# One re-searched instruction order for a 3x3 convolution with 2x2 max-pooling: head casts and evacuations on other engines, four stores cut into halves

## The chip, the core and the metric

The kernel runs on one core of one Trainium2 chip. The metric is device time in microseconds (us), as the median of several executions. The core has a matrix engine (TensorE, PE in the profile, with its weight loads as PEld), VectorE (DVE), ScalarE (ACT), GpSimd (POOL) and SyncE (SP). Each engine takes its instructions from its own queue. [...]

## The reference

```python
batch, c_in, h, w, c_out, k = 16, 64, 64, 64, 128, 3
x_pad = np.pad(x, ((0, 0), (0, 0), (1, 1), (1, 1)))
for b, co, ci, kh, kw:                      # five nested loops
    conv[b, co] += weight[co, ci, kh, kw] * x_pad[b, ci, kh:kh+h, kw:kw+w]
output[b, c, i, j] = max of the 2x2 block of conv[b, c] at rows 2i, 2i+1 and columns 2j, 2j+1
```

Input and output are fp32: 16 images of 64 channels with 64x64 pixels in, 16 images of 128 channels with 32x32 pixels out.

## The kernel before

**Tiling.** Two images lie side by side on the 128 partitions (2 x 64 channels). The work is cut into 32 steps, numbered 0 to 31; a step is a quarter of one such pair, that is 16 input rows or 8 row pairs. Within a step, `h` is 0 or 1, one of the two images; a product of `h` uses 64 rows of the PE array, so products of both images run beside each other in the two halves of the array. Each product is three matmuls (the three column taps) with a moving operand of 64x512 or 64x504 elements into one PSUM tile `acc` of 128x512 fp32. There are eight such tiles ("banks"), all of PSUM, handed out by a queue `free`.

**Even and odd rows.** Of a row pair the kernel needs the larger of the two convolution rows only. So a bank `ta` gets what one row has for itself, a bank `tb` what the other has, the larger of both is taken first, and what both have in common is added after that. A step is of one of two types (`TYPES`):

- K (10 steps): the input is cast to bf16 (`kx`); products `PA1`, `PA2` fill `ta`, `PB1`, `PB2` fill `tb`, `PR` adds the common part from a row sum `KS`.
- W (22 steps): row differences `E` and `D` and a row sum `WS` are made of the fp32 input `wx`. `P2` fills `ta`, `SE` copies it to `tb`, `P0` adds to `ta`, `P3` to `tb`, `P1` adds the common part.

**The steps of the order**, as the texts below name them (`MX.31.1` is `MX` of step 31, image 1):

| step | line | engine | work |
|---|---|---|---|
| `EV` | 439, 441 | ACT | copies bank `ta` to `ev` in SBUF and frees it |
| `SE` | 451 | ACT | copies `ta` to `tb` |
| `MX` | 467 | DVE | `tb` = max(`tb`, `ev`) |
| `OD` | 471 | ACT | copies the odd columns of `tb` to `od` |
| `CM` | 477 | DVE | `o` = max(even columns of `tb`, `od`), frees `tb` |
| `ST` | 485, 487 | SP (`ST.31.0`: ACT) | store of `o` |
| `WS` | 339, 352, 360 | DVE | row sum: with the odd rows copied to PSUM by `XC` on ACT (`ODD_ROWS_IN_PSUM`), as a reduction (`SUM_BY_REDUCTION`), or from two SBUF operands |
| `E`, `D` | 372, 381 | POOL; `E` of `DIFF_ON_VECTOR` on DVE | row differences |
| `KS` | 320 | DVE | row sum of a K step |
| `L`, `LB`, `LK` | 112, 101 | SP; `LK` POOL | loads; `LB` and `LK.0.0` wait for an earlier DVE step |

**The head.** The nine taps of the weights (`wraw`) are cast and combined into seven blocks (D2, G0, D0, G2, GM, G1, GP). `g0`, `g1`, `g2`, `D2`, `D0`, `GS`, `GM`, `GP` compute them, `u..` on POOL copies one 64-column slot, `T..` transposes a block on PE into a bank (line 170), `V..` evacuates the bank into `wt` as bf16 (lines 182 to 188). Step 0 is loaded as fp32 in two parts (`kfirst`) and cast row parity by row parity (`XOa`, `XOb`, `XEa`, `XEb`, line 492); its products `F.k.part` are half products of both images. `X1` and `X2` cast the second quarter (`ksecond`). Step 1, the first W step, is computed in halves too: `Ea`, `Eb`, `Da`, `Db`, `G.k.part`, `SEa`, `SEb`. Which engine does a head step is set by `TURNED_BY_SCALAR`, `CAST_BY_SCALAR`, `TAPS_BY_VECTOR` and `SUMS_BY_GPSIMD`. Eight dummy matmuls (line 595) keep PE busy until the weights have come.

**The order.** The kernel does not let the framework schedule. A string `ORDER` names every step in program order; each engine executes its own steps in that order, and waits by semaphores for what they depend on. Products are queued in two lanes, one for each image, and are emitted in pairs as soon as both lanes hold one. Before, the string ends with

```
... OD.29.1 CM.29.0 OD.31.0 CM.29.1 OD.31.1 ST.29 CM.31.0 ST.31.0 CM.31.1 ST.31.1
```

Of the kernel before, what the change touches and what calls it, by code (L numbers as in the profile page):

```python
# [11 lines left out]
def kernel(  # L12
# [467 lines left out]
    def store(s, h=None):  # L480
        p, q = place[s]
        dst = out[2 * p : 2 * p + 2, :, q * R : (q + 1) * R, :].rearrange("b c h w -> c b (h w)")
        src = ot[s].rearrange("p b h w -> p b (h w)")
        if h is None:
            nc.sync.dma_start(out=dst, in_=src)
        else:
            (nc.scalar, nc.sync)[h].dma_start(out=dst[:, h : h + 1], in_=src[:, h : h + 1])
# [46 lines left out]
    for m in PRODUCTS:  # L534
        steps[m] = lambda s, h, m=m: product(m, s, h)

    ORDER = """
# [5 lines left out]
        SE.3.0 P1.1.0 MX.1.1 MX.2.1 PR.2.0 P0.3.1 EV.3.1 P3.3.1 OD.1.0 P1.1.1 L.16 L.17 P0.3.0 MX.3.1 P3.3.0
        OD.2.0 EV.3.0 ST.0 CM.2.0 PR.2.1 OD.1.1 E.4 CM.1.0 MX.3.0 P1.3.1 PA1.5.1 PA1.5.0 L.15 PB1.5.0 PA2.5.1
        OD.2.1 E.11 P1.3.0 PB2.5.0 XC.6 PA2.5.0 L.12 CM.1.1 OD.3.1 XC.4 CM.2.1 CM.3.1 P2.4.0 PA1.7.0 P2.4.1
        OD.3.0 WS.6 EV.5.1 PB1.5.1 E.6 CM.3.0 WS.4 PA2.7.0 SE.4.1 EV.5.0 PB2.5.1 KS.5 KS.7 SE.4.0 WS.9 P0.4.1
        MX.5.1 P0.4.0 PA1.7.1 ST.3 P3.4.1 LK.1.0 EV.4.1 MX.5.0 EV.7.0 P3.4.0 PA2.7.1 MX.4.1 XC.8 EV.4.0 PR.5.1
        PR.5.0 EV.7.1 P2.6.0 PB1.7.0 OD.5.1 E.8 MX.4.0 OD.5.0 P1.4.1 CM.5.1 P1.4.0 PB1.7.1 CM.5.0 OD.4.1 PB2.7.1
        D.6 P2.6.1 PB2.7.0 SE.6.0 D.9 P2.8.1 OD.4.0 CM.4.1 WS.8 P0.6.0 SE.6.1 P3.6.0 MX.7.1 MX.7.0 PR.7.0 P2.8.0
        PR.7.1 D.8 EV.6.0 CM.4.0 OD.7.1 MX.6.0 SE.8.1 P0.6.1 CM.7.1 P3.6.1 P1.6.0 E.9 EV.6.1 LK.1.1 P0.8.1 L.20  # L550
        P3.8.1 MX.6.1 P1.6.1 D.11 P2.9.0 OD.7.0 SE.8.0 P2.9.1 CM.7.0 EV.8.1 ST.5 P0.8.0 OD.6.0 SE.9.0 P3.8.0
        MX.8.1 OD.6.1 CM.6.0 P1.8.1 P0.9.0 CM.6.1 L.22 EV.8.0 SE.9.1 P2.11.0 KS.13 MX.8.0 P3.9.0 E.12 P1.8.0
        PA1.13.1 OD.8.1 PA2.13.1 L.19 EV.9.0 SE.11.0 CM.8.1 EV.13.1 L.24 D.12 P0.9.1 OD.8.0 P3.9.1 P2.12.1
        P0.11.0 P3.11.0 WS.11 PA1.10.1 PA2.10.1 MX.9.0 P1.9.0 EV.9.1 PA1.13.0 EV.11.0 ST.4 CM.8.0 XC.14 ST.2
        MX.9.1 OD.9.0 SE.12.1 MX.11.0 P1.9.1 P2.11.1 WS.14 PA2.13.0 P1.11.0 EV.10.1 P0.12.1 EV.13.0 PA1.10.0
        E.14 OD.9.1 CM.9.0 P2.14.0 OD.11.0 SE.11.1 WS.12 CM.9.1 EV.12.1 P3.12.1 P0.11.1 D.14 PB1.10.1 CM.11.0
        E.15 P3.11.1 PA2.10.0 E.19 SE.14.0 EV.11.1 P2.12.0 KS.10 MX.12.1 E.17 PB2.10.1 L.23 P1.12.1 P0.14.0
        SE.12.0 MX.11.1 P1.11.1 P3.14.0 EV.14.0 XC.22 MX.14.0 EV.10.0 P0.12.0 WS.22 P2.14.1 MX.10.1 ST.1 P3.12.0
        E.20 EV.12.0 P1.14.0 OD.14.0 MX.12.0 PB1.13.1 OD.12.1 OD.11.1 PB1.10.0 CM.14.0 PB2.10.0 ST.6 P1.12.0
        CM.12.1 PB2.13.1 E.16 CM.11.1 PR.10.1 SE.14.1 P0.14.1 PA1.21.0 MX.13.1 ST.11 XC.17 PR.13.1 OD.12.0  # L560
        OD.10.1 P3.14.1 EV.14.1 PA2.21.0 MX.10.0 OD.13.1 CM.12.0 P2.15.1 EV.21.0 PR.10.0 D.15 D.16 P2.15.0
        CM.10.1 WS.17 CM.13.1 PA1.18.0 MX.14.1 PA2.18.0 OD.10.0 SE.15.0 P2.16.1 CM.10.0 WS.16 WS.15 P0.15.0
        SE.15.1 P3.15.0 SE.16.1 P1.14.1 PB1.13.0 EV.18.0 P0.15.1 OD.14.1 EV.15.0 P0.16.1 P3.15.1 KS.18 EV.15.1
        LK.2.0 CM.14.1 P2.16.0 ST.12 MX.15.0 ST.14 MX.15.1 P3.16.1 D.17 P2.17.1 EV.16.1 P1.15.1 PB2.13.0 MX.16.1
        SE.16.0 SE.17.1 P1.16.1 P1.15.0 P0.17.1 OD.15.0 P0.16.0 L.28 L.25 MX.13.0 P3.17.1 OD.15.1 EV.16.0
        PR.13.0 PA1.18.1 OD.16.1 P3.16.0 OD.13.0 D.20 WS.20 CM.15.1 EV.17.1 PA2.18.1 P2.17.0 CM.16.1 MX.16.0
        SE.17.0 P2.20.1 CM.13.0 P2.19.0 MX.17.1 EV.18.1 P1.17.1 P1.16.0 P0.17.0 CM.15.0 P3.17.0 OD.16.0 SE.20.1
        PA1.21.1 PB1.18.0 EV.17.0 SE.19.0 CM.16.0 ST.9 WS.19 OD.17.1 D.19 P0.20.1 EV.20.1 PA2.21.1 PB2.18.0
        MX.17.0 MX.18.0 E.24 P0.19.0 E.22 P3.20.1 P1.17.0 P2.19.1 EV.21.1 EV.19.0 CM.17.1 PR.18.0 PB1.18.1 E.23
        P3.19.0 MX.20.1 OD.17.0 OD.18.0 P2.20.0 ST.8 P1.20.1 SE.19.1 WS.23 OD.20.1 CM.17.0 P2.23.0 CM.18.0  # L570
        PB2.18.1 MX.19.0 SE.20.0 P1.19.0 L.30 P0.19.1 MX.18.1 EV.19.1 D.23 P3.19.1 OD.19.0 CM.20.1 KS.21 P0.20.0
        D.22 PR.18.1 P2.22.1 SE.23.0 P3.20.0 ST.10 CM.19.0 MX.19.1 PB1.21.1 EV.20.0 MX.20.0 OD.18.1 P0.23.0
        P1.19.1 P3.23.0 D.25 SE.22.1 CM.18.1 P1.20.0 PB2.21.1 EV.23.0 L.27 OD.19.1 P2.22.0 MX.23.0 P0.22.1
        CM.19.1 P1.23.0 OD.20.0 D.24 CM.20.0 MX.21.1 PB1.21.0 ST.15 SE.22.0 P2.23.1 P0.22.0 PB2.21.0 EV.22.1
        P3.22.1 E.25 PR.21.1 WS.28 OD.23.0 ST.19 CM.23.0 SE.23.1 EV.22.0 P2.24.0 P3.22.0 ST.17 P0.23.1 MX.22.1
        OD.21.1 EV.23.1 P3.23.1 MX.21.0 ST.16 P1.22.1 MX.23.1 CM.21.1 PR.21.0 SE.24.0 P2.24.1 OD.22.1 P0.24.0
        OD.21.0 P1.23.1 P2.25.1 CM.22.1 SE.24.1 P3.24.0 P0.24.1 OD.23.1 MX.22.0 EV.24.0 P1.22.0 CM.21.0 CM.23.1
        ST.21 WS.24 SE.25.1 P3.24.1 OD.22.0 CM.22.0 EV.24.1 P0.25.1 P3.25.1 ST.22 PA1.26.0 PA2.26.0 MX.24.1
        PA1.26.1 P2.25.0 EV.26.0 PB1.26.0 D.27 PA2.26.1 E.27 KS.26 PB2.26.0 WS.25 EV.25.1 SE.25.0 P2.27.1
        MX.25.1 P0.25.0 MX.26.0 EV.26.1 EV.25.0 MX.24.0 E.28 SE.27.1 P3.25.0 P1.25.1 PR.26.0 P1.24.0 P2.27.0  # L580
        ST.7 OD.25.1 MX.25.0 P1.24.1 P0.27.1 D.28 P3.27.1 OD.26.0 OD.24.1 P2.28.1 PB1.26.1 CM.25.1 OD.24.0
        CM.26.0 EV.27.1 CM.24.1 SE.27.0 P1.25.0 P2.28.0 P0.27.0 CM.24.0 OD.25.0 P3.27.0 PB2.26.1 WS.27 CM.25.0
        SE.28.1 P0.28.1 SE.28.0 P0.28.0 MX.27.1 E.30 P1.27.1 MX.26.1 PR.26.1 EV.27.0 L.31 P2.30.1 EV.28.1
        EV.28.0 E.31 OD.27.1 D.30 P3.28.0 ST.25 MX.27.0 OD.26.1 P3.28.1 MX.28.0 ST.24 P1.27.0 CM.27.1 CM.26.1
        P2.30.0 OD.27.0 CM.27.0 PA1.29.1 SE.30.1 P1.28.0 OD.28.0 PA2.29.1 MX.28.1 D.31 PA1.29.0 SE.30.0 CM.28.0
        ST.26 PA2.29.0 ST.13 EV.29.1 P2.31.0 P0.30.1 WS.31 P0.30.0 EV.29.0 ST.18 WS.30 P1.28.1 P3.30.0 PB1.29.0
        EV.30.1 P2.31.1 ST.20 OD.28.1 CM.28.1 EV.30.0 PB1.29.1 P3.30.1 KS.29 SE.31.0 MX.30.0 PB2.29.1 PB2.29.0
# [50 lines left out]
```

## Time and profile before

| | |
|---|---|
| median of 3 runs | 104.52 us (104.48 to 104.57) |
| the profiled execution | 104.47 us; its span from first to last instruction 102.7 us |
| granted TensorE clock | 1.000 |
| PE, DVE, ACT, POOL busy | 96.2, 91.6, 85.5, 77.9 us |
| matmuls | 905 (of them 870 of the convolution, 25 transposes) |
| DMA | 23.60 MB in all; HBM read 17.14 MB, written 8.39 MB |

Times in the profile are counted from the first instruction of the span. A row of a timeline gives the start, the duration, the engine, the line of the kernel, the operation, output and input by their names in the program, and how many instructions are merged into the row; in square brackets stands how long the engine sat idle before, and who ended that. Consecutive instructions of DVE overlap by some 0.08 us and of ACT by 0.1 us, so the distance from start to start is shorter than the duration.

### The profile page before, as it was taken

The numbers are of one execution on the slowest core, as the hardware profiler recorded it, in microseconds if no ns is written. First come the engines' busy times: TensorE is split into PE (matmuls) and PEld (weight loads), VectorE is DVE, ScalarE is ACT, GpSimd is POOL, SyncE is SP. The second block draws the span as 40 slices with busy tenths as digits, with TensorE's granted clock in tenths as the row PEclk, the third lists the DMA queues.
The fourth block names the chain that finished last, engine by engine and source line by source line (L and its number), as shares of the span: only waits on it lengthen the run. The fifth ranks groups of instructions, "written<-read, shape, count | busy, mean of one in ns | idle before, by whom it ended". The sixth has DMA issues, their size and how long they took to land.

```text
span 102.7 us, 2522 instructions
## 1 busy us (share of the span) xinstructions
PE 96.2 (94%) x905; PEld 54.3 (53%) x905; DVE 91.6 (89%) x176; ACT 85.5 (83%) x192; POOL 77.9 (76%) x66
## 2 busy tenths in 40 slices
...
GB/s 53 286 295 333 281 325 360 362 421 410 293 311 410 311 308 396 220 6 0 175 57 119 245 259 404 389 111 0 307 3 112 216 165 113 106 295 222 208 192 114
DMA packets 13341, 23.60 MB, mean 230 GB/s; under 512 B 1040, under 2 KB 9360, under 8 KB 13328
## 3 DMA queue, kind: packets, MB, share of 16 engines
...
q0 software_dynamic: 720, 2.10, 11.6%
q8 instruction: 7, 0.11, 0.5%
q10 hardware_dynamic: 144, 0.13, 0.4%
q14 instruction: 6, 0.05, 0.1%
HBM read 17.14 MB, written 8.39 MB: 249 GB/s over the span
## 4 chain that ended last, share of the span: by engine, by line
PE 88%; DMA 4%; DVE 2%; SPq 1%; issue 1%; ACT 0%; DVEq 0%
PE acc L219 86%; DMA kfirst<-in_x_dram 4%; DVE o L477 1%; PE acc L170 1%; DVE acc L467 1%; PE acc L460 1%; SPq L119 0%; ACT kx L492 0%; SPq L115 0%; DVEq L633 0%
## 5 line engine op out<-in xcount | busy, mean ns | idle before, releaser
L219 PEld LDWEIGHTS <-wt 64*128 64x128 bf16 x870 | 51.7, 94 | 39.0 <-issue 2.0
L219 PE MATMUL acc<-wd,wt 64*128 64x504 bf16 (+3 forms) x276 | 54.4, 367 | 0.0
L381 POOL TENSOR_TENSOR wd<-wx 128x1024 bf16<-128x1024 f32 x21 | 49.2, 2360 | 4.5 <-DVE ws L360 2.0
L219 PE MATMUL acc<-kx,wt 64*128 64x504 bf16 (+6 forms) x264 | 44.7, 355 | 0.9 <-DVE wq L508 0.7
L467 DVE TENSOR_TENSOR acc<-acc,ev 128x512 f32<-128x512 f32 x64 | 42.0, 691 | 1.2 <-ACT ev L441 0.7
L219 PE MATMUL acc<-we,wt 64*128 64x512 bf16 (+3 forms) x138 | 32.5, 367 | 0.0
L219 PE MATMUL acc<-ws,wt 64*128 64x512 bf16 (+1 forms) x132 | 32.5, 377 | 0.0
L441 ACT ACTIVATE ev<-acc 128x512 f32<-128x512 f32 x44 | 26.3, 614 | 1.8 <-PE acc L219 1.3
L451 ACT COPY acc<-acc 128x512 f32<-128x512 f32 x42 | 24.5, 591 | 3.0 <-PE acc L219 1.8
L477 DVE TENSOR_TENSOR o<-acc,od 128x256 f32<-128x256 f32 x64 | 24.7, 416 | 0.9 <-ACT od L471 0.9
L471 ACT COPY od<-acc 128x256 f32<-128x256 f32 x64 | 22.8, 382 | 2.2 <-PE acc L219 1.7
L372 POOL TENSOR_TENSOR we<-wx 128x512 bf16<-128x512 f32 x16 | 20.1, 1272 | 4.0 <-PE acc L219 2.4
L219 PE MATMUL acc<-ks,wt 64*128 64x504 bf16 (+1 forms) x60 | 13.7, 377 | 0.0
L439 ACT COPY ev<-acc 128x512 f32<-128x512 f32 x20 | 11.7, 593 | 1.3 <-PE acc L219 1.2
L352 DVE TENSOR_REDUCE ws<-wx 128x512 bf16<-128x1024 f32 x9 | 11.1, 1232 | 0.0
L360 DVE TENSOR_TENSOR ws<-wx 128x512 bf16<-128x512 f32 x7 | 5.3, 766 | 0.0
L320 DVE TENSOR_TENSOR ks<-kx 128x512 bf16<-128x512 bf16 x10 | 4.3, 435 | 0.0
L408 POOL TENSOR_TENSOR wd<-wx 128x512 bf16<-128x512 f32 x2 | 2.5, 1264 | 2.2 <-DVE we L393 2.2
L339 DVE TENSOR_TENSOR ws<-wx,acc 128x512 bf16<-128x512 f32 x6 | 4.1, 675 | 0.0
L595 PE MATMUL acc<-const-bfloat16-1.0 128*128 128x512 bf16 x8 | 3.3, 582 | 0.8 <-PEq L619 0.8
L335 ACT COPY acc<-wx 128x512 f32<-128x512 f32 x6 | 3.6, 598 | 0.1
L372 DVE TENSOR_TENSOR we<-wx 128x512 bf16<-128x512 f32 x4 | 2.9, 749 | 0.3 <-DMA wx<-in_x_dram 0.3
...
## 6 DMA issues: line engine op xcount, KB each, us to landing
...
```

The lines of the kernel that those rows point to most:

```text
L219: nc.tensor.matmul(acc[t][:, i0:i1, o0:o1], wt[lo : lo + CI, tap_of(m0, kw, h), :], rows(lo, i0, i1, c0, c1), start=start and kw == 1, sto ...
L320: nc.vector.tensor_tensor(out=row["ks", s], in0=t[:, f : f + 2 * R : 2, :], in1=t[:, f + 1 : f + 2 * R : 2, :], op=ADD)
L352: nc.vector.tensor_reduce(out=row["ws", s], in_=t[:, f : f + 2 * R, :].rearrange("p (r two) w -> p r w two", two=2), axis=mybir.AxisListTy ...
L360: nc.vector.tensor_tensor(out=row["ws", s], in0=t[:, f : f + 2 * R : 2, :], in1=t[:, f + 1 : f + 2 * R : 2, :], op=ADD)
L372: inst = (nc.vector if vector else nc.gpsimd).tensor_tensor(out=row["we", s], in0=t[:, f : f + 2 * R : 2, :], in1=t[:, f + 1 : f + 2 * R : ...
L381: nc.gpsimd.tensor_tensor(out=row["wd", s], in0=t[:, f + 1 : f + 1 + 2 * R, :], in1=t[:, f - 1 : f - 1 + 2 * R, :], op=SUB)
L439: nc.scalar.copy(out=ev[s, h], in_=acc[t])
L441: nc.scalar.mul(ev[s, h], acc[t], -1.0)
L451: nc.scalar.copy(out=acc[t], in_=acc[ta[s, h]])
L467: nc.vector.tensor_tensor(out=t, in0=t, in1=ev[s, h], op=MAX)
L471: nc.scalar.copy(out=od[s, h], in_=acc[tb[s, h]][:, :, 1::2])
L477: nc.vector.tensor_tensor(out=ot[s][:, h], in0=acc[t][:, :, 0::2], in1=od[s, h], op=MAX)
```

## The change

Three things change; the computation, the sizes and the number of each operation on PE stay the same.

First, steps move between engines. In the head, `g1` and `g2` go from DVE to ACT, the sum `GP` from POOL to DVE, the casts `XOb` and `XEb` from ACT to DVE, the evacuations `VG0` and `VGM` from ACT to DVE and `VD0` from DVE to ACT. Later, `E.20` goes from POOL to DVE and `E.19` from DVE to POOL; one row sum more is a reduction (ten instead of nine, of other steps), and step 12 instead of 14 has its odd rows copied to PSUM.

Second, steps 8, 12, 16 and 20 are stored as two transfers of 128 KB instead of one of 256 KB; all these go by SP, and `ST.31.0` alone stays on ACT.

Third, `ORDER` is another permutation of the steps. The hunks of the settings and of the stores are complete; of the order, the head, a stretch in the middle and the end are shown.

```diff
-    DIFF_ON_VECTOR = (3, 8, 9, 15, 19,)
+    DIFF_ON_VECTOR = (3, 8, 9, 15, 20,)
-    SUM_BY_REDUCTION = (1, 3, 11, 12, 19, 20, 24, 28, 31,)
-    ODD_ROWS_IN_PSUM = (4, 6, 8, 14, 17, 22,)
-    TURNED_BY_SCALAR = ("G0", "GM", "G1", "GP",)
-    CAST_BY_SCALAR = ("XEa", "XOa", "XEb", "XOb",)
-    TAPS_BY_VECTOR = ("g1", "g2",)
-    SUMS_BY_GPSIMD = ("GP",)
+    SUM_BY_REDUCTION = (1, 3, 11, 14, 15, 19, 23, 24, 30, 31,)
+    ODD_ROWS_IN_PSUM = (4, 6, 8, 12, 17, 22,)
+    TURNED_BY_SCALAR = ("D0", "G1", "GP",)
+    CAST_BY_SCALAR = ("XEa", "XOa",)
+    TAPS_BY_VECTOR = ()
+    SUMS_BY_GPSIMD = ()
...
-            (nc.scalar, nc.sync)[h].dma_start(out=dst[:, h : h + 1], in_=src[:, h : h + 1])
+            queue = nc.scalar if s == N - 1 and h == 0 else nc.sync
+            queue.dma_start(out=dst[:, h : h + 1], in_=src[:, h : h + 1])
...
-        g0 D2 TD2 XOa g2 GS TG0 VD2 D0 XOb XEb TG2 g1 F.0.0 F.0.1 TD0 uG1 GM VG0 GP XEa F.1.0 F.1.1 VD0 F.2.0
-        uGM EV.0.1 TG1 F.2.1 uGP LB.3 VG2 LK.0.0 TGM X1 LB.4 F.3.0 TGP X2 KS.0 L.11 PA1.2.0 LB.6 Ea F.3.1 VGM
-        LB.9 PA1.2.1 KS.2 EV.0.0 VG1 PA2.2.1 Eb LB.8 MX.0.1 Da G.0.0 MX.0.0 G.0.1 VGP PR.0.1 SEa.1 SEa.0 Db
+        D2 D0 g1 g0 TD2 uG1 XOa g2 GS TG0 VD2 VG0 XOb TD0 GM F.0.0 GP TG1 XEa F.1.0 F.0.1 VD0 TG2 F.2.0 XEb
+        F.2.1 LB.3 X2 F.1.1 uGM uGP VG2 LB.6 LB.4 KS.0 TGM LK.0.0 VGM X1 F.3.1 EV.0.0 TGP EV.0.1 PA1.2.0 F.3.0
+        L.11 PA1.2.1 LB.9 Ea L.12 KS.2 Eb VGP VG1 G.0.0 PA2.2.0 G.0.1 SEa.0 MX.0.1 SEa.1 Da SEb.1 PR.0.1 MX.0.0
...
+        ST.0 ST.7 CM.12.1 EV.12.0 MX.10.1 L.27 OD.11.1 PB2.10.0 MX.12.0 PR.10.1 CM.11.1 P1.14.0 XC.22 P1.12.0
+        SE.14.1 D.15 MX.10.0 PB2.13.1 PR.10.0 PA1.21.0 P0.14.1 OD.14.0 WS.22 E.17 OD.10.1 CM.14.0 PA2.21.0
+        OD.12.0 OD.10.0 EV.14.1 P3.14.1 MX.13.1 PR.13.1 P2.15.0 CM.10.1 CM.10.0 CM.12.0 E.19 XC.17 PA1.18.0 ST.2
+        EV.21.0 P2.15.1 MX.14.1 PA2.18.0 WS.17 OD.13.1 P1.14.1 D.16 L.24 CM.13.1 E.20 WS.16 SE.15.0 SE.15.1
+        P2.16.1 P0.15.1 P3.15.0 ST.11 OD.14.1 EV.18.0 P0.15.0 P2.16.0 PB1.13.0 SE.16.1 P3.15.1 CM.14.1 EV.15.1
+        P0.16.1 EV.15.0 PB2.13.0 P2.17.1 P3.16.1 WS.15 MX.15.1 SE.16.0 MX.15.0 D.17 P1.15.1 EV.16.1 P0.16.0
+        SE.17.1 LK.2.0 P0.17.1 P3.16.0 EV.16.0 OD.15.1 EV.17.1 WS.20 E.23 MX.16.1 P3.17.1 MX.13.0 D.19 CM.15.1
+        P1.16.1 P1.15.0 MX.16.0 P2.17.0 OD.15.0 PR.13.0 CM.15.0 OD.16.1 PA1.18.1 P1.16.0 CM.16.1 PA2.18.1
...
-        MX.29.1 MX.31.0 MX.31.1 OD.30.0 CM.30.0 OD.30.1 PR.29.0 P1.31.0 PR.29.1 CM.30.1 ST.23 OD.29.0 P1.31.1
-        ST.30 OD.29.1 CM.29.0 OD.31.0 CM.29.1 OD.31.1 ST.29 CM.31.0 ST.31.0 CM.31.1 ST.31.1
+        MX.29.1 EV.31.0 EV.31.1 PR.29.0 P1.30.1 OD.30.0 PR.29.1 OD.30.1 MX.31.0 MX.31.1 P1.31.0 OD.29.0 CM.30.0
+        P1.31.1 CM.30.1 OD.29.1 CM.29.0 CM.29.1 ST.30 OD.31.0 CM.31.0 ST.29 ST.31.0 OD.31.1 CM.31.1 ST.31.1
```

More of the change, by code (lines that the diff above doesn't have):

```diff
@@ L537 @@
     ORDER = """
-        g0 D2 TD2 XOa g2 GS TG0 VD2 D0 XOb XEb TG2 g1 F.0.0 F.0.1 TD0 uG1 GM VG0 GP XEa F.1.0 F.1.1 VD0 F.2.0
-        uGM EV.0.1 TG1 F.2.1 uGP LB.3 VG2 LK.0.0 TGM X1 LB.4 F.3.0 TGP X2 KS.0 L.11 PA1.2.0 LB.6 Ea F.3.1 VGM
-        LB.9 PA1.2.1 KS.2 EV.0.0 VG1 PA2.2.1 Eb LB.8 MX.0.1 Da G.0.0 MX.0.0 G.0.1 VGP PR.0.1 SEa.1 SEa.0 Db
-        SEb.0 WS.1 PA2.2.0 L.14 SEb.1 PR.0.0 EV.2.1 G.1.0 E.3 OD.0.0 CM.0.0 G.1.1 EV.2.0 EV.1.0 G.2.1 G.2.0 WS.3
-        OD.0.1 LK.0.1 MX.1.0 P2.3.1 PB1.2.1 PB1.2.0 D.3 EV.1.1 PB2.2.0 SE.3.1 P2.3.0 PB2.2.1 CM.0.1 D.4 MX.2.0
@@ L543 @@
[L543 to L587, printed above, removed]
@@ new lines @@
+        L.11 PA1.2.1 LB.9 Ea L.12 KS.2 Eb VGP VG1 G.0.0 PA2.2.0 G.0.1 SEa.0 MX.0.1 SEa.1 Da SEb.1 PR.0.1 MX.0.0
+        SEb.0 PA2.2.1 WS.1 OD.0.1 PR.0.0 Db OD.0.0 LB.8 LK.0.1 G.1.0 G.1.1 E.3 G.2.1 CM.0.1 PB1.2.0 PB2.2.0 L.14
+        EV.2.0 G.2.0 EV.1.0 P2.3.1 EV.1.1 EV.2.1 PB1.2.1 D.3 WS.3 PB2.2.1 MX.1.0 CM.0.0 D.4 P2.3.0 MX.2.0 L.15
+        SE.3.1 MX.1.1 P0.3.1 E.4 P1.1.0 MX.2.1 P3.3.1 PR.2.0 SE.3.0 P1.1.1 EV.3.1 P0.3.0 PR.2.1 OD.2.0 OD.1.0
+        MX.3.1 EV.3.0 P3.3.0 OD.1.1 P1.3.1 PB1.5.0 OD.2.1 CM.2.0 PA1.5.1 CM.1.0 E.6 PB2.5.0 E.11 XC.6 MX.3.0
@@ new lines @@
+        P1.3.0 PA2.5.1 P2.4.1 OD.3.1 XC.4 CM.2.1 PB1.5.1 L.20 CM.1.1 PA1.5.0 OD.3.0 CM.3.1 WS.6 CM.3.0 PA2.5.0
+        SE.4.1 PB2.5.1 WS.4 P2.4.0 KS.5 EV.5.1 P0.4.1 P3.4.1 WS.9 KS.7 EV.5.0 PA1.7.1 PA1.7.0 MX.5.0 SE.4.0
+        PA2.7.0 EV.4.1 P0.4.0 P3.4.0 EV.7.0 LK.1.0 LK.1.1 XC.8 MX.5.1 ST.3 PR.5.0 EV.4.0 PA2.7.1 EV.7.1 L.19
+        PR.5.1 OD.5.0 MX.4.1 E.8 MX.4.0 OD.5.1 P2.6.0 P1.4.1 CM.5.0 D.6 OD.4.1 CM.5.1 PB1.7.1 PB1.7.0 PB2.7.1
+        P2.6.1 SE.6.0 CM.4.1 WS.8 P1.4.0 P0.6.0 OD.4.0 PB2.7.0 MX.7.1 P2.8.1 SE.6.1 EV.6.0 PR.7.1 P0.6.1 P3.6.0
@@ new lines @@
+        OD.7.1 CM.4.0 MX.7.0 D.9 ST.5 SE.8.1 P2.8.0 EV.6.1 PR.7.0 P3.6.1 D.8 P0.8.1 L.16 P3.8.1 OD.7.0 MX.6.0
+        P1.6.0 SE.8.0 CM.7.1 E.9 ST.4 EV.8.1 OD.6.0 MX.6.1 P2.9.0 P1.6.1 P0.8.0 CM.7.0 P2.9.1 MX.8.1 P3.8.0
+        SE.9.0 OD.6.1 EV.8.0 P1.8.1 P0.9.0 CM.6.0 E.12 D.11 P2.11.0 CM.6.1 MX.8.0 SE.9.1 PA1.13.1 EV.9.0 P3.9.0
+        ST.6 P1.8.0 P0.9.1 PA2.13.1 OD.8.1 WS.11 SE.11.0 E.14 P0.11.0 EV.9.1 P3.9.1 CM.8.1 P2.12.1 L.17 P3.11.0
+        MX.9.0 OD.8.0 D.12 XC.12 L.25 CM.8.0 L.22 EV.11.0 PA1.10.1 P1.9.0 PA2.10.1 EV.13.1 MX.9.1 PA1.13.0
@@ new lines @@
+        OD.9.0 P1.9.1 WS.12 MX.11.0 SE.12.1 CM.9.0 EV.10.1 L.23 P2.11.1 PA2.13.0 P1.11.0 WS.14 P0.12.1 OD.9.1
+        CM.9.1 EV.13.0 P2.14.0 OD.11.0 SE.11.1 CM.11.0 D.14 PA1.10.0 PA2.10.0 SE.14.0 P3.12.1 KS.18 P0.11.1
+        EV.12.1 EV.11.1 P2.12.0 KS.10 E.15 E.16 P0.14.0 P3.11.1 P3.14.0 MX.12.1 PB1.10.1 SE.12.0 P1.12.1 P0.12.0
+        EV.14.0 P3.12.0 ST.9 PB1.10.0 PB2.10.1 MX.11.1 P1.11.1 KS.13 OD.12.1 EV.10.0 P2.14.1 MX.14.0 PB1.13.1
+        ST.0 ST.7 CM.12.1 EV.12.0 MX.10.1 L.27 OD.11.1 PB2.10.0 MX.12.0 PR.10.1 CM.11.1 P1.14.0 XC.22 P1.12.0
```

23 lines of the change are left out of this document (22 added, 1 removed).

## The prediction

> **What bounds the kernel now.** I read the page first, then the chain of waits in order of time.
>
> ```profile
> PE 96.2 (94%) x905; PEld 54.3 (53%) x905; DVE 91.6 (89%) x176; ACT 85.5 (83%) x192; POOL 77.9 (76%) x66
> ...
> PE 88%; DMA 4%; DVE 2%; SPq 1%; issue 1%; ACT 0%; DVEq 0%
> ```
>
> ```profile
> 1.65 4.30 DMA kfirst<-in_x_dram
> 5.95 0.02 issue
> 5.98 0.41 ACT kx L492
> 6.39 0.04 issue
> 6.43 0.50 PE acc L219 x6
> ...
> 12.27 84.18 PE acc L219 x785
> ...
> 96.50 0.69 DVE acc L467
> ...
> 98.09 0.75 DVE o L477 x2
> ```
>
> The kernel has three parts: a head that ends when PE starts for good at 6.43, a body in which PE goes through, and a tail of DVE and ACT after the last matmuls. In the body a pair of products starts every 0.648 us; from F.0.1 at 6.43 to the last pair at 96.92 no pair starts late. In that last pair, P1.31.1 waits 0.13 us for MX.31.1. So the body can't get shorter: the number of matmuls stays. The change can win at the two ends only, and it loses wherever its new order makes PE wait.
>
> The table by windows shows how near that is:
>
> ```profile
> 40.00:50.00 10.00, 10.00 (x96) 6.05 (x94) 10.00 (x20) 9.23 (x22) 8.38 (x6) 1.00 0.34 125
> 50.00:60.00 10.00, 10.00 (x95) 5.46 (x92) 10.00 (x20) 8.94 (x22) 8.86 (x5) 1.00 0.75 143
> ```
>
> The third pair of numbers is DVE: it is as full as PE for 20 us. The tail, in the timeline:
>
> ```profile
> 97.75 1.41 DVE L477 TENSOR_TENSOR o<-acc,od 128x256 f32<-128x256 f32 x4
> ...
> 97.88 0.65 ACT L471 COPY od<-acc 128x256 f32<-128x256 f32 x2
> 98.86 0.37 ACTq L487 DMA_DIRECT2D out_dram<-o  x1
> 99.19 0.34 SPq L487 DMA_DIRECT2D out_dram<-o  x1
> ```
>
> The row of ACT holds OD.31.0 and OD.31.1, back to back, done at 98.53. The last two CM of DVE end at 98.83 (CM.31.0) and 99.16 (CM.31.1). ST.31.0 is issued by ACT at 98.86, as the last thing that ACT does, ST.31.1 by SP at 99.19; they land at 101.34 and 101.52. From there to the end of the span it is 1.1 us of closing work, which nothing here touches. The profiled execution took 104.47 us, 1.8 more than its span and 0.05 under the median; the sum is made against 104.47.
>
> **The head: a gain of 0.25.**
>
> ```profile
> 5.76 0.50 PE L219 MATMUL acc<-kx,wt 64*128 64x256 bf16 x6 [0.70 <-DVE wq L508]
> 6.43 0.50 PE L219 MATMUL acc<-kx,wt 64*128 64x256 bf16 x6 [0.16 <-ACT kx L492]
> ```
>
> F.0.0 starts when XOa is done: the load lands at 5.29, XOa takes 0.41 on ACT, 5.76. That stays. Then PE idles until XOb lets F.0.1 go at 6.43. After the change TG1 and F.1.0 stand there, which need nothing of XOb: uG1 and g1 are done by 4.7, VG0 by 5.5 (DVE: D2 3.59, D0 4.01, VD2 4.70, VG0 5.1). With start-to-start distances of the trace (half product to transposes 0.44, transposes to half product 0.27 or 0.36, half product to half product 0.26 to 0.33, product pair 0.65), PE runs: TG1 6.20, F.1.0 6.47, F.0.1 6.73 (XOb on DVE from 5.97, done about 6.3), TG2 7.17, F.2.0 7.53 (VD0 on ACT done about 7.0), F.2.1 7.85 (XEb behind XOb, GM and GP on DVE, done about 7.4), F.1.1 8.18, TGM 8.61, F.3.1 8.89, TGP 9.32, F.3.0 9.60, PA1.2 9.94 (X1 done 9.65), end 10.58. Before, the pair PA1.2 started at 10.26. Now one new wait: G.0.0 needs the banks that EV.0.0 and EV.0.1 free, and on ACT these now come behind X2 and X1, which wait for a load that lands at 8.49:
>
> ```profile
> 8.51 1.14 ACT L501 CAST kx<-ksecond 128x512 bf16<-128x512 f32 x2
> ```
>
> Two EV at 0.58 behind it end at 10.62, so G.0.0 starts at 10.66 instead of 10.91, and G.1.0 at 13.26 instead of 13.51. Casts on DVE have no row; bounds are 0.2 and 0.5 (the 192-element cast takes 0.49), and any value fits, since F.0.1 and F.2.1 have 0.4 us to spare. g1, g2, GP, VG0, VGM and VD0 change engines inside idle stretches (DVE idled 0.74 and 0.93 us there, ACT 1.19); if that cover went, each would cost its own 0.35 to 0.6.
>
> Loads: LB.3 now waits for XEb (7.4) instead of GM (6.56). It is covered, because the transfers ahead of it keep the queue busy until 9.90; it landed at 13.20, E.3 started there, and D.3 behind it ends at 16.36. P0.3.1, then at 16.53, needs D.3: 0.12 to spare, and what LB.3 lands later than that comes off the gain. LB.4 now goes behind LB.6 and lands near 17.1 instead of 15.0; D.4 and E.4 (2.36 and 1.27) on POOL then end at 20.7, for P2.4.1 at 21.07. I take 0 for both. LK.1.1, moved ahead of D.6 on POOL, delays it by 0.6 where POOL idled 1.4 us for a row sum of DVE. The four extra issues on SP (0.37 each) lie in a queue that waits 52 us for DVE; loads behind them are needed over 5 us later.
>
> **The body: a loss of 0.15.** One more row sum is a reduction:
>
> ```profile
> L352 DVE TENSOR_REDUCE ws<-wx 128x512 bf16<-128x1024 f32 x9 | 11.1, 1232 | 0.0
> L360 DVE TENSOR_TENSOR ws<-wx 128x512 bf16<-128x512 f32 x7 | 5.3, 766 | 0.0
> ```
>
> That is 1.23 - 0.77, or 0.47 us more on DVE. Where DVE is full it decides. From MX.10.0 to CM.16.1 the new order puts on DVE: 8 MX at 0.598, 9 CM at 0.332, 2 row sums with PSUM at 0.595, one reduction at 1.147 and three with two SBUF operands at 0.70 (start to start; these range from 0.60 to 0.91, longer beside POOL), together 12.21. PE has 19 pairs between PB2.10.0, which lets MX.10.0 start, and PA1.21.1, which needs the bank of CM.16.1: 12.32. Add 0.21 from PE's slot to a reader's start (as for EV.31.0 at 95.18) and 0.13 for the end of CM and the start of PE: 12.55, so PE waits 0.23. The same count over the old order gives nothing above 0 but 0.22 at the last pair, where the trace has 0.13. So I take 0.15; with 0.60 it is 0, with 0.91 it is 0.86. At the end, WS.30 as a reduction costs 0.24 more, but KS.29 and CM.28.1 are moved ahead, and MX.29.0 waits for PE either way.
>
> **The tail: a loss of 0.74.** On ACT, ST.31.0 now stands ahead of OD.31.1. ST.31.0 waits for CM.31.0 on DVE, whose queue up to there is the same eight steps as before. So with the old times: CM.31.0 ends 98.83, ST.31.0 is issued from 98.86 to 99.24, and only then OD.31.1 runs (0.37, start 0.04 behind): 99.65. It was done at 98.53. CM.31.1 follows (0.03 + 0.43): 100.11, and ST.31.1 is issued at 100.13 instead of 99.19: 0.94 later. It then lands alone: ST.30, alone in the queue, took 2.11 from issue to landing, ST.31.1 behind its neighbours 2.33. So the loss is 0.72 to 0.94; I take 0.74, near the lone store. What waits behind the waiting store is OD.31.1, for it DVE's last CM, and for that the last store: nothing else is left to hide it.
>
> A rule of the Trainium skill stands against the size of this. DMA: Bandwidth & Descriptors, section Issuing engines are not separate DMA queues, calls the sequencer's time to initiate a DMA usually small relative to the DMA; the row has 0.37 against 2.3. Taken as nothing, the tail would lose 0.35.
>
> Sum: 104.47 - 0.25 + 0.15 + 0.74 = 105.11.
>
> **The rivals.**
>
> - *Wait without issue* (0.10): the issue runs beside ACT's next instruction, only the wait holds it. OD.31.1 starts at 98.90, ST.31.1 0.57 later than before, less 0.22: a loss of 0.35 to 0.57 and 104.7 to 104.9. For it: no row of this trace has an ACT instruction behind an ACT issue. Against it: on SP consecutive issues start one duration apart (1.18, 1.65).
> - *No hold* (0.20): ACT passes OD.31.1 to its compute pipe although the store ahead of it waits. The place is ACT's queue at 98.3; it decides if OD.31.1 starts before CM.31.0 ends. Then the tail costs 0: 104.37 with the body's loss, 104.22 without, which is faster. For it: the trace shows ACT's sequencer working ahead, with the semaphore step of ST.31.0 at 98.09, before OD.31.1 starts at 98.15. Against it: that step stands ahead of OD.31.1 by 0.07 only, and the issue itself came 0.03 after CM.31.0. TensorE: Matmul & The Clock Gate of the Trainium skill, section Architectural detail, has ACT as strict FIFO; no run here shows it yet.
> - *DVE becomes the bound* (0.12): the three two-operand sums meet POOL at 0.91 each and the body loses 0.86: 104.47 - 0.25 + 0.86 + 0.74 = 105.82. For it: both engines stand at 10.00. Against it: their mean is 0.70.
>
> **How the numbers follow.** My forecast has 0.58 and lies between 104.95 and 105.6 by the bounds of head, body and landing. A measurement of this kernel tells apart about 0.2%, 0.21 us: faster is under 104.31, slower over 104.73. No hold is split into faster 0.12 and same 0.08; the other cases make slower 0.80. The range from 104.3 leaves out the best of no hold, and up to 105.9 it takes in the third rival's 105.82.
>
> **What would show it.** Right: F.1.0 before F.0.1 at 6.47; G.1.0 near 13.26; PE's first late pair near P1.16.0 or PA1.21.1; in the tail about 0.7 us between the starts of OD.31.0 and the store, and OD.31.1 behind the row ACTq L487; the last CM alone, some 0.8 us behind the one before. Wrong: OD.31.1 ahead of the store's issue, or a stall of PE in the first 20 us, which would be LB.3 or LB.4 landing late.

## The result, and the profile after

The kernel after takes 105.09 us (median of 15 runs, 104.43 to 105.72), the kernel before 104.52 beside it (median of 15): a ratio of 1.0044, 95% interval 1.0025 to 1.0063. By that ratio it is slower by 0.46 us; the medians differ by 0.57, because the ratio leaves out two executions of before (106.65 and 106.76 us) that ran in a slower state of the chip. The forecast was 105.1. The total is right; of its terms the body was too small, the tail too large, and a gain at the very end was not seen, so part of the agreement is luck. The profiled execution of after took 104.89 us, its span 103.1 (before 104.47 and 102.7).

The page's busy times and the shares of the chain:

```profile
PE 97.4 (95%) x905; PEld 52.8 (51%) x905; DVE 92.7 (90%) x178; ACT 85.3 (83%) x191; POOL 77.8 (75%) x65
...
PE 93%; DVE 2%; issue 1%; ACT 0%; ACTq 0%
```

The chain of waits in order of time (start, us, what):

```profile
12.07 50.79 PE acc L219 x477
62.86 0.04 issue
62.90 33.77 PE acc L219 x308
...
99.08 0.37 ACTq L488
...
99.49 0.38 ACT od L471
...
99.89 0.42 DVE o L477
```

Two things are new against before. PE's one long stretch of 84.18 us is broken at 62.86: there PE waited. And the end now runs over ACT's queue, the issue of a store, then one `OD`, then one `CM`; before it ran over DVE alone.

Set beside each other, with the boundaries G.1.0, the start of the last product (P1.31.1, at 97.24 before and 97.46 after) and the last landing:

| stretch | before | after | difference | predicted |
|---|---|---|---|---|
| head, to G.1.0 | 13.51 | 13.31 | -0.20 | -0.25 |
| body, to the last product | 83.73 | 84.15 | +0.42 | +0.15 |
| tail, to the last store's landing | 4.28 | 4.76 | +0.48 | +0.74 |
| closing work | 1.14 | 0.90 | -0.24 | 0 |
| span | 102.66 | 103.11 | +0.46 | +0.64 |

**Head.** PE's timeline:

```profile
5.57 0.82 PE L219 MATMUL acc<-kx,wt 64*128 64x256 bf16 x6
6.32 0.38 PE L170 MATMUL acc<-ident,wq 128*128 128x128 bf16 x3
6.64 0.75 PE L219 MATMUL acc<-kx,wt 64*128 64x192 bf16 x12
```

F.0.0, then TG1, then F.1.0 and F.0.1 in one row: the gap behind F.0.0 is filled as forecast, and no row shows an idle time.

**Body.** The table by windows (PE, PEld, DVE, ACT, POOL, then clock and DMA):

```profile
40.00:50.00 10.00, 10.00 (x96) 5.63 (x94) 10.00 (x21) 8.97 (x22) 8.10 (x6) 1.00 1.01 337
50.00:60.00 10.00, 10.00 (x95) 5.07 (x93) 10.00 (x19) 9.45 (x22) 7.86 (x5) 1.00 0.68 181
60.00:70.00 10.00, 9.96 (x93) 4.91 (x89) 9.55 (x18) 8.71 (x20) 9.45 (x6) 1.00 0.40 125
```

DVE is full from 40 to 60 us as before, and PE does not fall short there. It falls short from 60 to 70, where DVE has air and POOL is fullest. POOL's timeline says why:

```profile
53.21 2.36 POOL L381 TENSOR_TENSOR wd<-wx 128x1024 bf16<-128x1024 f32 x1 [1.29 <-DVE ws L360]
55.50 0.58 POOL L101 DMA_DIRECT2D kx<-in_x_dram  x1
56.92 1.27 POOL L372 TENSOR_TENSOR we<-wx 128x512 bf16<-128x512 f32 x1 [0.85 <-PE acc L219]
58.16 7.00 POOL L381 TENSOR_TENSOR wd<-wx 128x1024 bf16<-128x1024 f32 x3
65.14 1.26 POOL L372 TENSOR_TENSOR we<-wx 128x512 bf16<-128x512 f32 x1
66.37 2.35 POOL L381 TENSOR_TENSOR wd<-wx 128x1024 bf16<-128x1024 f32 x1
```

These rows are D.17, LK.2.0, E.23, then D.19, D.20 and D.22, then E.22 and D.23. D.20 ends at 62.84; P0.20.1 starts at 62.90, 0.21 late. D.23 ends at 68.72; P0.23.0 starts at 68.77, 0.24 late. Before, the steps D.17, D.20 and D.19 ran in one row, and D.20 started at 56.28:

```profile
53.95 6.99 POOL L381 TENSOR_TENSOR wd<-wx 128x1024 bf16<-128x1024 f32 x3 [1.14 <-DVE ks L320]
```

Now D.17 waits for a row sum, then E.23 waits for WS.20, and E.23, which PE needs only at 66.58 (P2.23.0), stands ahead of D.19 and D.20. The row of E.23 names a matmul as what ended the idle time. But POOL's own step that waits for DVE was done at 56.38, 0.04 behind the end of WS.20 (56.34), and e3 below shows that E.23 can start at 56.18 when it need not wait for WS.20.

**Tail.** The timeline:

```profile
99.08 0.37 ACTq L488 DMA_DIRECT2D out_dram<-o  x1
99.49 0.37 ACT L471 COPY od<-acc 128x256 f32<-128x256 f32 x1 [1.02 <-DVE o L477]
99.89 0.42 DVE L477 TENSOR_TENSOR o<-acc,od 128x256 f32<-128x256 f32 x1 [0.84 <-ACT od L471]
```

OD.31.1 idled 1.02 us behind the waiting store, the last CM 0.84 us behind OD.31.1, and ST.31.1 is issued 2.89 us after the last product starts instead of 1.95: +0.94.

### The profile page after: what moved, and what is told of

Its sections match the earlier page's. It is cut to its first block, busy times and chain, and to the rows that moved or that the text cites. A ratio compares the mean times of both kernels' runs of the same rounds, so it can differ in the third digit from the quotient of the medians.

```text
span 103.1 us, 2533 instructions
## 1 busy us (share of the span) xinstructions
PE 97.4 (95%) x905; PEld 52.8 (51%) x905; DVE 92.7 (90%) x178; ACT 85.3 (83%) x191; POOL 77.8 (75%) x65
## 4 chain that ended last, share of the span: by engine, by line
PE 93%; DVE 2%; issue 1%; ACT 0%; ACTq 0%
PE acc L219 87%; PE acc L596 3%; PE acc L170 2%; DVE o L477 2%; DVE acc L467 1%; PE acc L460 1%; ACT od L471 0%; ACTq L488 0%
## 5 line engine op out<-in xcount | busy, mean ns | idle before, releaser
L219 PEld LDWEIGHTS <-wt 64*128 64x128 bf16 x870 | 49.7, 94 | 40.5 <-issue 2.0
L219 PE MATMUL acc<-wd,wt 64*128 64x504 bf16 (+3 forms) x276 | 53.3, 367 | 0.0
L219 PE MATMUL acc<-kx,wt 64*128 64x504 bf16 (+6 forms) x264 | 47.1, 358 | 0.0
L219 PE MATMUL acc<-ks,wt 64*128 64x504 bf16 (+1 forms) x60 | 14.6, 377 | 0.0
L352 DVE TENSOR_REDUCE ws<-wx 128x512 bf16<-128x1024 f32 x10 | 12.3, 1233 | 0.0
L360 DVE TENSOR_TENSOR ws<-wx 128x512 bf16<-128x512 f32 x6 | 4.4, 740 | 0.0
L157 POOL COPY wq<-wq 128x64 bf16<-128x64 bf16 x3 | 1.1, 388 | 3.6 <-ACT wq L194 1.9
L101 POOL DMA_DIRECT2D kx<-in_x_dram x5 | 3.0, 591 | 1.0 <-DVE ks L320 1.0
```

The lines of the kernel that those rows point to most:

```text
L219: nc.tensor.matmul(acc[t][:, i0:i1, o0:o1], wt[lo : lo + CI, tap_of(m0, kw, h), :], rows(lo, i0, i1, c0, c1), start=start and kw == 1, sto ...
L352: nc.vector.tensor_reduce(out=row["ws", s], in_=t[:, f : f + 2 * R, :].rearrange("p (r two) w -> p r w two", two=2), axis=mybir.AxisListTy ...
```

## The experiments

Each kernel ran in turn with the kernel before on one chip. The median of the kernel before differed from one comparison to the next (104.52, 104.60, 104.90, 104.83, 105.05), so what counts is the ratio. e8 rests on 5 executions and e3 on 6, the others on 12 or 13.

| kernel | us | ratio to before | 95% interval |
|---|---|---|---|
| after | 105.09 | 1.0044 | 1.0025 to 1.0063 |
| e1, OD.31.1 first | 104.51 | 0.9989 | 0.9963 to 1.0015 |
| e2, the hold put into before | 105.42 | 1.0078 | 1.0044 to 1.0111 |
| e3, E.23 ahead of WS.20 | 106.12 | 1.0150 | 1.0112 to 1.0188 |
| e4, the head's gap back | 105.45 | 1.0067 | 1.0035 to 1.0099 |
| e5, GpSimd's order | 105.00 | 1.0006 | 0.9982 to 1.0029 |
| e6, WS.23 of two operands | 105.63 | 1.0059 | 1.0029 to 1.0089 |
| e7, last store on SP | 104.83 | 1.0006 | 0.9980 to 1.0031 |
| e8, three edits | 104.16 | 0.9924 | 0.9908 to 0.9940 |
| e9, L.12 behind LB.8 | 105.20 | 1.0035 | 1.0004 to 1.0065 |
| e10, split stores in before | 104.84 | 0.9985 | 0.9954 to 1.0016 |
| e11, after again | 105.48 | 1.0066 | 1.0033 to 1.0100 |
| e12, three edits and LB.4 | 104.36 | 0.9938 | 0.9907 to 0.9970 |

### The tail: e1, e2, e7

e1, in the kernel after:

```diff
-... ST.29 ST.31.0 OD.31.1 CM.31.1 ST.31.1
+... OD.31.1 ST.29 ST.31.0 CM.31.1 ST.31.1
```

> The changed kernel with one step moved: OD.31.1 ahead of ST.31.0 again, nothing else. Theory (the store holds ScalarE, and the end pays for it): OD.31.1 starts about 0.3 us behind OD.31.0, ST.31.1 is issued 2.3 us after the last product pair starts instead of 3.2. What of this reaches the end: the prediction's term says 0.74 us off the time (104.35 from 105.09); read from the two profiles, where the lone last store landed in 1.87 instead of 2.33 us and the closing work was 0.24 us shorter, only 0.25 us (104.85). Rival (the end pays nothing, since landing and closing work take it back): 105.1, no change.

e2, in the kernel before:

```diff
-... OD.31.1 ST.29 CM.31.0 ST.31.0 CM.31.1 ST.31.1
+... ST.29 CM.31.0 ST.31.0 OD.31.1 CM.31.1 ST.31.1
```

> The kernel before with one step moved: ST.31.0 ahead of OD.31.1, as the change has it, nothing else. Theory: the last evacuation starts behind the store's issue, the last store is issued 0.95 us later; the time grows by 0.25 us if the shorter landing and closing work are as in the changed kernel's profile, by 0.74 us if they are as the prediction had it. Rival (the end pays nothing): the same time as before.

e7, in the kernel after:

```diff
-            queue = nc.scalar if s == N - 1 and h == 0 else nc.sync
+            queue = nc.sync
```

> The kernel after, with ST.31.0 at its place in the order, but issued by SyncE instead of ScalarE. Theory (the store's wait and issue in ScalarE's queue hold OD.31.1): OD.31.1 runs right behind OD.31.0 at about 98.4, CM.31.1 at about 99.0, ST.31.0 is issued at 99.1 and ST.31.1 at 99.5 instead of 100.35; by the run with the store behind OD.31.1 the time falls by 0.4 to 0.6, to 104.5 to 104.7, a ratio of 0.999 to 1.001. Rival (not the queue, the new order of steps is what delays the end): OD.31.1 stays at 99.5 and the time at 105.0 to 105.1, a ratio of 1.004.

Taking the hold away brings 0.55% (104.51); putting it into the kernel before, and nothing else, costs 0.78%, about 0.8 us with an interval of 0.35 on either side. In e2 ACT's timeline is that of after: the issue at 99.02, OD.31.1 at 99.44 behind 1.02 us of idle time, and ST.31.1 lands 1.89 after its issue:

```profile
99.02 0.37 ACTq L487 DMA_DIRECT2D out_dram<-o  x1
99.44 0.37 ACT L471 COPY od<-acc 128x256 f32<-128x256 f32 x1 [1.02 <-DVE o L477]
```

From the start of the last product to the last landing it is 4.78 us there, 0.50 more than in before, and the closing work stays at 1.15: the expectation's 0.25 counted on the shorter closing work of after, which e2 does not have. In e1 the closing work stays short (0.90) and the tail is back at 4.28, so in the profiles the hold is worth 0.48 to 0.50, within the interval of both times.

In e7 the store keeps its place in the order but leaves ACT. In its profile (of an execution of 105.8 us, so all times are later) OD.31.1 starts at 99.79, right behind OD.31.0 at 99.52, and 0.38% come back. SP's queue is now the late one: ST.31.0 is issued at 100.63 and ST.31.1 only at 101.17, 0.38 after the end of its CM. That did not lengthen the tail: from the last product to the last landing it is 4.27, and 4.28 in e1. The 0.38% here and the 0.55% of e1 can't be told apart. So it is the queue that holds, not the place in the order as such.

### The body on GpSimd: e3, e5, e6

e3, in the kernel after:

```diff
-... WS.20 E.23 MX.16.1 ...
+... E.23 WS.20 MX.16.1 ...
```

> The changed kernel with two neighbours of the order swapped: E.23 (GpSimd) ahead of WS.20 (VectorE), so that E.23 no longer waits for WS.20; the order on VectorE, ScalarE and PE stays. Theory (the body's loss of 0.41 us is GpSimd late: E.23 starts at 56.92 only, and behind it D.20 ends at 62.84 and D.23 at 68.72, for which PE waits 0.21 and 0.24 us): E.23 starts 0.4 to 0.8 us earlier, both late pairs are gone or nearly so, 0.2 to 0.45 us off the time. Rival (VectorE is full and the late pairs are its own, as the prediction had it): E.23 is earlier, the pairs near 62.5 and 68.8 stay late, and the time is the same.

E.23 does start earlier, at 56.18, and the kernel loses 1 us more. Rows of DVE and of POOL:

```profile
55.74 2.27 DVE L360 TENSOR_TENSOR ws<-wx 128x512 bf16<-128x512 f32 x1
...
56.18 1.28 POOL L372 TENSOR_TENSOR we<-wx 128x512 bf16<-128x512 f32 x1
```

WS.20, a sum of two SBUF operands, took 2.27 us instead of 0.68 and ended 0.56 behind E.23; MX.16.1 and CM.16.1 behind it came as much later, and P1.16.1, which needs MX.16.1, started 1.09 late. That is the price that the program avoids where `on_gpsimd` makes a row difference wait for the last such operation of DVE.

e5 moves nothing on DVE:

```diff
-... WS.20 E.23 MX.16.1 ... PA2.21.1 D.20 OD.16.0 ... EV.17.0 D.22 P0.19.0 EV.21.1 E.22 ... CM.20.1 D.23 ST.15
+... WS.20 MX.16.1 ... PA2.21.1 D.20 E.23 OD.16.0 ... EV.17.0 P0.19.0 EV.21.1 E.22 ... CM.20.1 D.23 D.22 ST.15
```

> The kernel after, with GpSimd's row differences in another order: D.19, D.20, E.23, E.22, D.23, D.22 instead of E.23, D.19, D.20, D.22, E.22, D.23. Nothing else is changed. Theory (the body is lost on GpSimd): without E.23 ahead, D.20 ends at about 61.6 instead of 62.84 and D.23 at about 66.5 instead of 68.72; P0.20.1 and P0.23.0 need them at 62.5 and 68.5, so both late pairs (0.21 and 0.24) are gone, and the time falls by 0.3 to 0.45, to 104.65 to 104.8, a ratio to the kernel before of 1.000 to 1.003. Rival (VectorE is what bounds the body, as the prediction had it): VectorE's rows are as full as before, PE's wait turns up elsewhere, and the time stays at 105.0 to 105.1, a ratio of 1.004.

The two late pairs are gone and 0.38% with them, which is just clear of the noise (the interval of the difference is 0.30 on either side). D.20 now follows D.19 at once and ends at 62.11:

```profile
57.43 4.68 POOL L381 TENSOR_TENSOR wd<-wx 128x1024 bf16<-128x1024 f32 x2 [0.43 <-DVE ws L360]
```

DVE has the same work, so it was not what bounded the body. The profile of e5 (of an execution of 105.5 us) showed another loss, though; its chain in order of time:

```profile
11.89 12.17 DMA wx<-in_x_dram
...
24.15 0.13 DVE ws L360
...
28.54 0.58 ACT acc L451
29.11 0.05 issue
29.16 68.01 PE acc L219 x627
```

From 29.16 PE runs through to the end, which no profile of after does. But up to there the chain hangs on a load: LB.8 landed at 24.06 (23.01 in the first profile of after, 22.17 before), WS.9 waited 0.9 us for it, and PE lost 0.69.

e6 makes the added reduction a plain sum again:

```diff
-    SUM_BY_REDUCTION = (1, 3, 11, 14, 15, 19, 23, 24, 30, 31,)
+    SUM_BY_REDUCTION = (1, 3, 11, 14, 15, 19, 24, 30, 31,)
```

> The kernel after, with the row sum WS.23 made from two operands instead of as a reduction. By the prediction's step for the body (a reduction costs 0.47 us more on a full VectorE, from which it took 0.15) the time falls by 0 to 0.15, to 104.95 to 105.1, a ratio of 1.003 to 1.004. Theory (a sum of two SBUF operands and a GpSimd row difference hold each other up, as in the run with E.23 ahead of WS.20, where the sum took 2.27 us): WS.23 meets D.20 on GpSimd; it takes 2.0 to 3.0 us instead of 1.24, or D.20 starts 0.6 late; D.22, which then has to wait for it, and D.23 come later, and the time rises by 0.5 to 1.7, to 105.6 to 106.8, a ratio of 1.009 to 1.021.

The profile (of an execution of 106.82 us, longer than the median of 105.63) shows WS.23 at 0.71 us instead of 1.24, and D.20, which DVE's sum here got ahead of, at 2.84 instead of 2.36: P0.20.1 was 0.69 late instead of 0.21. The saving on DVE bought nothing, and POOL paid 0.48. Most of what makes this execution long lies elsewhere: between 20 and 30 us PE lost 1.4 us to late loads. The ratio, 1.0059, lies between both expectations and does not decide alone.

### The head: e4

```diff
-... F.0.0 GP TG1 XEa F.1.0 F.0.1 VD0 ...
+... F.0.0 GP XEa F.0.1 TG1 F.1.0 VD0 ...
```

> The changed kernel with TG1 and F.1.0 put behind F.0.1 again, as the old order has it. Theory (the head's gain comes from work put into the wait for the second part of the input): PE waits idle for XOb, G.1.0 starts 0.2 to 0.35 us later than in the changed kernel (13.31) and the time grows by as much, to 105.3. Rival (the head is set by the weights' or the input's arrival and the slower first matmuls, not by this order): G.1.0 within 0.1 us of 13.31 or moved with the landings only, no change in time.

PE stands idle again ahead of F.0.1, for 0.19 us. The time does not show what that costs: the ratio is 1.0067, but the unchanged kernel, compared again (e11), reads 1.0066. Two profiles show it. In e8 the order is the filled one and the two parts of `kfirst` land at 5.62 and 6.36, in e4 at 5.59 and 6.39; G.1.0 starts at 13.47 in e8 and at 13.81 in e4. With the same landings the filled gap is worth 0.34 there.

### The loads: e9, e11

e9, in the kernel after:

```diff
-... LB.9 Ea L.12 KS.2 ... OD.0.0 LB.8 LK.0.1 ...
+... LB.9 Ea KS.2 ... OD.0.0 LB.8 L.12 LK.0.1 ...
```

> The kernel after with one load moved: L.12 behind LB.8 in SyncE's queue instead of ahead of KS.2. Theory (in many executions LB.8, now behind L.12, lands after 23.2 and WS.9 and then PE wait, as in the profiles with OD.31.1 first and with the other GpSimd order, where LB.8 landed at 23.57 and 24.06 and PE lost 0.28 and 0.64): LB.8 lands about 1.4 us earlier, PE has no late pair between 20 and 30 us, and the time falls by 0.15 to 0.4, to 104.7 to 104.95 at the level of the first comparison, a ratio of 1.001 to 1.003. Rival (the late landing comes of the profiling or is rare): the time stays within 0.1 of the kernel after.

> The kernel after, unchanged, beside the two others on the same chip, so that their differences from it need no comparison through an earlier one. Expected: a ratio of 1.003 to 1.006. By the theory of the late load, its profile shows either LB.8 landed after 23.2 and a late pair of PE between 20 and 30 us, or neither.

With e11 as the comparison e9 gains 0.31%, with the first comparison of after 0.09%; the intervals overlap, so the time does not show it. What the profiles show is the landing: with L.12 behind it LB.8 landed at 21.98 in e9 and at 21.49 in e8, with L.12 ahead of it between 23.01 and 24.54 in the eight profiles that have that order. In e9 no pair is late from 20 to 30 us, but none was in the first profile of after either. e11 loses 0.40 there, and it came to it by another way than expected. Rows of POOL and of DVE:

```profile
17.53 2.38 POOL L381 TENSOR_TENSOR wd<-wx 128x1024 bf16<-128x1024 f32 x1 [1.08 <-DMA wx<-in_x_dram]
...
22.89 1.00 DVE L320 TENSOR_TENSOR ks<-kx 128x512 bf16<-128x512 bf16 x1
23.86 0.69 DVE L360 TENSOR_TENSOR ws<-wx 128x512 bf16<-128x512 f32 x1
```

LB.4, which the change put behind LB.6, landed at 17.46, and D.4 waited 1.08 for it. E.11, three steps later on POOL, therefore ran until 23.61, into the time of KS.5, another sum of two SBUF operands, which took 1.00 instead of 0.42. WS.9, CM.4.1 and P2.6.1 followed late. In the first profile of after LB.4 had landed at 16.11, 0.02 ahead of the end of D.3: there was no slack at all.

### The closing work: e10

The stores of steps 8, 12, 16 and 20 cut in two in the kernel before, all on SP.

```diff
-            (nc.scalar, nc.sync)[h].dma_start(out=dst[:, h : h + 1], in_=src[:, h : h + 1])
+            (nc.scalar if s == N - 1 and h == 0 else nc.sync).dma_start(out=dst[:, h : h + 1], in_=src[:, h : h + 1])
...
-... ST.12 ... ST.8 ... ST.16 ... ST.20 ...
+... ST.12.0 ST.12.1 ... ST.8.0 ST.8.1 ... ST.16.0 ST.16.1 ... ST.20.0 ST.20.1 ...
```

> The kernel before with the stores of steps 8, 12, 16 and 20 cut image by image, all on SyncE, and nothing else. Theory (SyncE tests the stores' semaphores in a fixed order at the end, some 0.06 us for each pair; with four more transfers the last store's semaphore comes last in that order instead of fourth from last of eight): the four tests behind the last landing run while it is in flight, the work from the last landing to the end of the span is 0.87 us instead of 1.11, and the time falls by 0.24, a ratio of 0.9975 to 0.998. Rival (the four issues more on SyncE and the smaller transfers delay stores and loads behind them, and the shorter closing work in the kernel after comes of its late last store): 0 to 0.2 slower, a ratio of 1.000 to 1.002.

Inconclusive in time: 0.9985 takes in both expectations. The trace shows the mechanism, though its execution took 107.08 us where the median is 104.84; the closing work is not the part that was longer. The stores use eight semaphores in turn, and at the end SP tests them in seven instructions of fixed order, 0.061 us apart. Before, ST.31.1's semaphore is tested at 101.54, right after its landing, and four more tests follow, to 101.81. With four transfers more, it is the last in the turn: in after, e1, e8 and e10 nothing is left to test behind the last landing. From landing to the end of the span it is 1.14 in before and 1.15 in e2, but 0.90, 0.89, 0.90 and 0.91 in after, e1, e8 and e10.

### A version that beats both: e8, e12

e8 is the kernel after with the edits of e1, e5 and e9; e12 moves LB.4 ahead of LB.6 as well.

> The kernel after with three edits: OD.31.1 ahead of ST.31.0 (0.58 in the run with that alone), GpSimd's order as in e5 (0.3 to 0.45), and the load L.12 behind LB.8, which in one profile of these kernels landed at 23.57 and made WS.9 wait 0.6 us (0 to 0.3). If the parts add up: 103.95 to 104.25, a ratio to the kernel before of 0.994 to 0.997, faster than both kernels. Rival (the parts do not add: once GpSimd is not late, VectorE is, which has no slack between 40 and 62 us): 104.4 to 104.6, a ratio of 0.998 to 1.000.

> The kernel with all three edits, and LB.4 ahead of LB.6 in SyncE's queue, as it was before the change. Theory (loads that land late reach PE by two ways: LB.8 through WS.9, and LB.4 through D.4; in the run of the kernel after beside the two others LB.4 landed at 17.46, D.4 waited 1.08 for it, E.11 behind it ran until 23.61, KS.5 beside it took 1.00 instead of 0.42, and PE lost 0.28): LB.4 lands at 13.5 to 15, D.4 starts behind D.3, no pair of PE is late between 20 and 30 us, and the time stays at or a little under that of the kernel with three edits, 103.9 to 104.2, a ratio of 0.990 to 0.994. Rival (the run with three edits was short by chance, its five executions not telling): 104.4 to 104.8, a ratio of 0.996 to 1.000.

Both are faster than either kernel, at 0.9924 and 0.9938. Between the two nothing can be told apart. The parts add up: off 1.0055, the mean of the two comparisons of after, e1, e5 and e9 bring 0.66, 0.49 and 0.20%, which leaves 0.992. The chain of e12:

```profile
12.68 84.17 PE acc L219 x785
```

PE runs through once more, as in before (84.18). Its start at 12.68 is late because the second part of `kfirst` landed at 6.98 in this execution.

## Why the prediction was right, and where it was not

**Head, -0.25: right in mechanism** (e8 beside e4: 0.34), and -0.20 in the profile. F.1.0 stood ahead of F.0.1, at 6.64 instead of 6.47, and G.1.0 started at 13.31 (13.26 forecast). That the size came so near is in part luck, for two deviations went against each other: the first part of `kfirst` landed at 4.44 and not at 5.29, so F.0.0 started at 5.57 and not at 5.76, but it took 0.75 to the next start and not 0.44.

**Body, +0.15: wrong engine, and too small.** The failed step is the sum over DVE from MX.10.0 to CM.16.1. It priced one more reduction at 0.47 on the fullest engine and put the first late pair near P1.16.0 or PA1.21.1. No pair was late there. The three sums of two SBUF operands took 0.66, 0.60 and 0.60 from start to start, not 0.70, and with 0.60 the prediction's own count gives no wait: MX.16.0 ended at 58.48 and P1.16.0 started at 58.59, so DVE had about 0.06 to spare. What failed beyond that size was the choice of chain: behind 21 us the prediction gave POOL's steps no due times, though the diff shows E.23 ahead of D.19. The body lost 0.42 in the profile, and the order on POOL is worth 0.40 by e5. The reduction's 0.47 was mis-valued too: the other form of the sum cost POOL 0.48 (e6) or DVE 1.6 (e3) in the two places where a row difference ran beside it.

**Loads, 0: mis-sized.** The step said that LB.4 would land near 17.1 and D.4 and E.4 end at 20.7 ahead of P2.4.1 at 21.07, and stopped there. It did not follow POOL's queue on to E.11 and to KS.5 beside it, and LB.8 behind L.12 was not looked at. In the first profile they landed just in time, LB.4 0.02 ahead of the end of D.3 and LB.8 0.09 ahead of WS.9; in e11, e1, e7, e5 and e6 PE lost 0.40, 0.44, 0.59, 0.69 and 1.41 us between 20 and 30 us.

**Tail, +0.74: the mechanism exact, the landing mis-sized.** The delay of the issue was forecast as 0.94 and is 0.94, step by step: the store's issue 0.37, OD.31.1 0.04 behind it, CM.31.1, ST.31.1. But the lone last store took 1.87 from issue to landing (2.33 before), not the 2.11 of ST.30: that row is of a store of two images, twice the bytes. So the tail to the landing cost 0.48, outside the 0.72 to 0.94 of the prediction. e1 puts the hold at 0.57, e2 at 0.8. One sign was misread: the prediction wanted about 0.7 us between the starts of OD.31.0 and the store, but it is 0.98 (98.10 to 99.08), and it was 0.98 before as well (97.88 to 98.86). The closing work, "which nothing here touches", became 0.24 shorter, through the second part of the change, the halved stores, which the prediction treated as four issues more.

**The rivals.** *Wait without issue* and *no hold* are both refuted by one row: OD.31.1, whose input was complete when the last matmul of P1.31.1 ended at 98.26, starts at 99.49, 0.04 behind the end of the store's issue. The strict order of ACT that the Trainium skill states (TensorE: Matmul & The Clock Gate, Architectural detail) agrees with the 1.02 us of idle time there. By its other rule (DMA: Bandwidth & Descriptors, Issuing engines are not separate DMA queues) initiating is usually small beside the DMA itself. The 0.37 is small beside the 2.45 from issue to landing of ST.31.0 (99.08 to 101.53), but at the end of a kernel it lies on the path in full. *DVE becomes the bound* is refuted by e5.

**Why sums and differences get in each other's way.** In e6 DVE's sum came first and POOL's row took 2.84; in e11 POOL's E.11 came first and KS.5 took 1.00; in e3 WS.20 started 0.44 ahead of E.23, and yet it was WS.20 that took 2.27. The Trainium skill, SBUF — State Buffer, section Who interferes with whom, says that a DVE operation with two SBUF inputs contends with a GpSimd operation that reads SBUF, that a reduction does not, and that issue order decides who blocks. The first two rows agree, and so does the reduction in after: WS.23 took 1.24 beside D.20 at 2.36. In the third POOL was busy issuing LK.2.0 (55.59 to 56.16) when WS.20 began; whether that counts as POOL being first, no run here separates. That issue alone did not slow the sum: in after WS.20 began 0.16 into the same issue (55.66 against 55.50) and took 0.68. Nor is it settled why E.23 in after starts 0.58 behind the end of WS.20, where other row differences follow such a sum by 0.08 to 0.23.
